# Conditioning vectors of the first feed-forward in column quarters instead of halves

## The chip, the cores and the metric

The kernel runs on one core of a Trainium2 chip. The metric is the device time of one execution in microseconds (us); the time given for a kernel is the median of its runs. A profile is of one execution, taken by the hardware profiler. Engines: PE multiplies matrices, DVE and ACT work on vectors, POOL too, SP issues the loads to the DMA engines.

## The reference

One inference step of a two-layer decoder trunk for a prompt group of 512 tokens and a sample group of 8 sequences of 4 tokens. Each layer is a feed-forward, a mixer and a second feed-forward; each of these three reads a normalised and modulated copy of the residual stream:

```python
mod = (silu(c) @ w_ada[layer] + b_ada[layer]).reshape(Bn, 3, 3, 1024)
u = rmsnorm(h, g_norm[layer, 0]) * (1 + mod[:, 0, 1]) + mod[:, 0, 0]     # scale and shift
h = h + 0.5 * mod[:, 0, 2] * ((silu(a) * b) @ w_down)                      # a, b = split(u @ w_up)
```

`c` is one row per sequence (9 in all), `w_ada` has 1024 rows and 9216 columns. The first feed-forward cannot begin before its shift and scale, two vectors of 1024 numbers for each of the 9 rows, are made from two blocks of `w_ada` of 1024 x 1024 float32 (4.2 MB each).

## The kernel before

The stream `h` lies transposed, as 8 blocks of 128 features by 544 tokens (512 of the prompt, 32 of the samples). Tokens go in two halves of 272. A product is made of three multiplications of float32r parts (high by high, high by low, low by high), lines 176 to 178; the parts are made by a cast on ACT (L157) and a subtraction on DVE (L158). The feed-forward is `ffn_seven`: 22 column blocks of 128 features, each with a pair of weight blocks, one for `a` and one for `b`. The first three column blocks go plainly, one bank of accumulators for each of the pair and each half of the tokens; the rest is done with seven products in place of eight, from sums of operands made on DVE, ACT and POOL. The other function, `ffn`, is called nowhere.

Conditioning vectors are numbered in the order of use; vector 0 is the first shift, vector 1 the first scale. All others go through `ada_steps`: eight loads of 512 KB of 128 full rows (L232), 64 multiplications and a turn (a copy by ACT, two transposes by PE, the addition of the bias and the like by DVE in `set_mods`), handed out one step at a time by `tick` in the feed-forwards. Their loads go into the four buffers of `ada_tile`. Vectors 0 and 1 are made in halves of their columns, `ada_half_loads` (L278), `ada_half` (L288) and `ada_half_turn` (L294 and L296): four loads of 512 KB for one half of one vector, in pieces of 512 columns (2 KB) of two row blocks. Since the memory of the products is not yet in use, their loads borrow the buffers of the product weights, in the order that the list `slots` names: four of `ada_tile`, four of the high and low parts, two raw ones, four more of the high and low parts, and two of `ada_tile` again.

The order of the work is a planner's: it takes the instructions in the order of the program and with its own costs writes one list for each engine, which that engine then runs in order. The loads are all issued by SP. SP's list at the start is: `c`, the identity, the tokens, the first half of vector 0 (with four small loads between), the pair of weight blocks for column block 0 (L163), the first half of vector 1 (with the other four small loads), the second halves of both, then the first four loads of vector 2 (L232), and then the weight pairs for column blocks 1 and 2. The small loads fill `vrow`, which is turned into `vec`, the biases and norm weights that `set_mods` needs.

`first_u(part)` turns one half of both vectors and then makes four blocks of the modulated stream, `make_u`, for both halves of the tokens: a scaling by DVE (L382), the high part by ACT (L401), the low part by DVE (L402), and for the sample tokens a few small operations on DVE, POOL and ACT. With the first half's four blocks, the products of the pair of column block 0 can run over half of their depth; `feed()` then makes the second half, and the rest of the products follows. `tc.issue_after(ready)` holds back the products of the second half of the tokens on the first four blocks until the last conditioning multiplication is issued:

```python
part_of_bank(0, 0)
ready = feed()
with tc.issue_after(ready):
    part_of_bank(1, 0)
for half in range(2):
    part_of_bank(half, 1)
```

There are five banks for products; the pair takes four. The conditioning products of both halves lie in one bank of their own, at different columns.

Of the kernel before, what the change touches and what calls it, by code (L numbers as in the profile page):

```python
# [99 lines left out]
def trunk_kernel(ctx: ExitStack, tc: tile.TileContext, a, out, dbg=None, stop=None):  # L100
# [171 lines left out]
    def ada_half_loads(v, part, slots, between=None):  # L272
        w2d, c0 = ada_cols(v)
        c0 += 512 * part
        ts = []
        for k in range(0, NB, 2):
            t = slots.pop(0)(f"adah{v}_{part}_{k}")[:, 0:1024].rearrange("p (k c) -> p k c", k=2)
            SP.dma_start(out=t, in_=w2d[k * P:(k + 2) * P, c0:c0 + 512].rearrange("(k p) c -> p k c", p=P))  # L278
            ts.append(t)
            if between:  # L280
                between()
        return ts

    def ada_half(v, part, ts, ps):
        o = P * (2 * part + v)
        for k in range(NB):
            for j in range(4):
                mm = PE.matmul(ps[32 * j:32 * j + 32, o:o + P], lhsT=sc[:, k, :], rhs=ts[k // 2][:, k % 2, j * P:(j + 1) * P], start=k == 0, stop=k == NB - 1)  # L288
        return mm

    def ada_half_turn(v, part, ps):
        o = P * (2 * part + v)
        rows = ap_.tile([P, 256], F32, tag="adar", name=f"adahr{v}_{part}")
        S.copy(rows[:, 0:P], ps[:, o:o + P])  # L294
        pt = aux_bank(f"adaht{v}_{part}")
        PE.transpose(pt[:, 0:P], rows[:, 0:P], ident)  # L296
        b = 8 * v + 4 * part
        set_mods(v, 4 * part, 4, mods[:, b:b + 4, :], pt[:, 0:P].rearrange("p (j r) -> p j r", j=4)[:, :, 0:9],
                 vec[:, b:b + 4].unsqueeze(2).to_broadcast([P, 4, 9]))
# [125 lines left out]


    def ffn(name, l, s, gate, after_half, steps=(), final=False, first=None, held=()):
        wu = a["w_ffn_up"][l, s]
        wd = a["w_ffn_down"][l, s]
        steps, held = list(steps), list(held)  # L430
        total, ticks = len(steps), [0]

        def tick():
            ticks[0] += 1
            due = total * ticks[0] // (2 * NQ) - (total - len(steps))
            for _ in range(due):
                steps.pop(0)()

        with tc.tile_pool(name="ffn" + name, bufs=1) as fp:
            gt, wt = {}, {}  # L440

            def up_tiles(q):
                if q not in gt:
                    if q not in wt:
                        wt[q] = (split_cols(f"ua{name}_{q}", wu, q * P), split_cols(f"ub{name}_{q}", wu, FF + q * P))
                    gt[q] = (fp.tile([P, T], F32R, tag="gh", name=f"gh{name}_{q}", bufs=6),
                             fp.tile([P, T], F32R, tag="gl", name=f"gl{name}_{q}", bufs=6))

            def up(q, half):
                up_tiles(q)  # L450
                pa = mm_bank(f"pa{name}_{q}_{half}")
                apply_u(pa, wt[q][0], half)
                pb = mm_bank(f"pb{name}_{q}_{half}")
                apply_u(pb, wt[q][1], half)
                gated(q, half, pa, pb)

            def gated(q, half, pa, pb):
                t0, t1 = HALF[half]
                g = fp.tile([P, HA], F32, tag="g", name=f"g{name}_{q}_{half}", bufs=3)
# [5 lines left out]
            def down(qs, last):  # L465
                wd2 = {}
                for q in qs:
                    _, hi, lo = split(f"wd{name}_{q}", lambda raw: [(raw[:, 0:D], wd[q * P:(q + 1) * P])], D)
                    wd2[q] = (hi, lo)
# [1457 lines left out]
```

## Time and profile before

| what | value |
|---|---|
| median of three runs | 2356.05 us (2349.58 to 2356.92) |
| the profiled execution | 2357.5 us |
| its span | 2355.7 us |
| mean granted clock of PE | 0.988 |
| DMA over the span | 319.43 MB, mean 136 GB/s |
| loads of vectors 0 and 1 (L278) | 16 of 512 KB |

A row of the order of time reads: start, duration, engine, line of the kernel, operation, what is written from what is read, shape, count, and in brackets how long the engine stood idle before it and what ended that. SPq is the queue of loads on SP; its duration is that of the issue, with what it waited for inside a group, and not of the transfer. A busy share of PE near full says that PE had instructions at work, not that it ran at its peak. The granted clock is a share of full speed.

### The profile page before, as it was taken

The page shows a single profiled execution, that of the slowest core. Times are in us where ns is not written, and L with a number is a line of the kernel's source. Part 1 is how long each engine was busy: PE and PEld are TensorE (multiplying, and loading weights), DVE is VectorE, ACT ScalarE, POOL GpSimd, SP SyncE. Part 2 cuts the span into 40 slices and gives each one's busy share as a digit, 9 for nine tenths or more (in the row PEclk, how much of TensorE's full clock was granted, in tenths as well). Part 3 has the DMA queues.
Part 4 walks back from the last instruction along what each step waited for, and adds up shares of the span by engine and source line. Part 5 has one row for each costly group of instructions (what it writes and reads, how often), then busy time and mean ns, then how long its engine had stood idle before and what let it go on. Part 6 is the DMA issues. An engine that isn't in the chain of part 4 may idle for free. (4 is left out here: it accounts for less than half of the span.)

```text
span 2355.7 us, 48935 instructions
## 1 busy us (share of the span) xinstructions
PE 2282.2 (97%) x19292; PEld 2129.1 (90%) x19292; DVE 1740.4 (74%) x3785; ACT 977.8 (42%) x1815; POOL 906.8 (38%) x912
## 2 busy tenths in 40 slices
PE   7999999998999999999989999999998999999999
PEld 6899999997979999999868999999896679999999
DVE  6877677639556976777695977888766767977785
ACT  3333333434533443333523444344436654444432
POOL 0354544206202354553232355552324222465541
PEclk8999999999999999999999999999999999999999
DMA  9545555322263436555458333233147741332331
GB/s 312 175 126 193 195 194 191 108 68 59 61 190 89 141 96 199 190 177 185 153 190 254 102 97 106 86 102 113 48 104 175 232 126 43 91 103 88 100 99 66
DMA packets 356635, 319.43 MB, mean 136 GB/s; under 512 B 24991, under 2 KB 317693, under 8 KB 356358
## 3 DMA queue, kind: packets, MB, share of 16 engines
q1 hardware_dynamic: 341478, 300.24, 40.7%
q0 software_dynamic: 14928, 16.06, 2.8%
q8 instruction: 152, 2.49, 0.4%
q14 instruction: 77, 0.63, 0.1%
HBM read 298.17 MB, written 18.38 MB: 134 GB/s over the span
## 5 line engine op out<-in xcount | busy, mean ns | idle before, releaser
L178 PE MATMUL pd<-gh,ld 128*128 128x272 f32 x1408 | 405.9, 288 | 2.3 <-DVE ld L158 2.3
L176 PE MATMUL pd<-gh,hd 128*128 128x272 f32 x1408 | 406.9, 289 | 1.4 <-ACT gh L157 1.4
L177 PE MATMUL pd<-gl,hd 128*128 128x272 f32 x1408 | 406.3, 289 | 1.6 <-DVE gl L158 1.2
L176 PE MATMUL p<-uh,hu 128*128 128x272 f32 x1216 | 351.5, 289 | 0.0
L178 PE MATMUL p<-uh,lu 128*128 128x272 f32 x1216 | 350.8, 288 | 0.0
L177 PE MATMUL p<-ul,hu 128*128 128x272 f32 x1216 | 350.4, 288 | 0.0
L178 PEld LDWEIGHTS pd<-gh,ld 128*128 128x128 f32 x1408 | 265.4, 189 | 3.0 <-DVE ld L158 3.0
L177 PEld LDWEIGHTS pd<-gl,hd 128*128 128x128 f32 x1408 | 265.6, 189 | 2.8 <-DVE gl L158 1.6
L176 PEld LDWEIGHTS pd<-gh,hd 128*128 128x128 f32 x1408 | 265.6, 189 | 2.1 <-ACT gh L157 1.6
L176 PE MATMUL p<-th,hu 128*128 128x272 f32 x912 | 264.2, 290 | 0.0
L178 PE MATMUL p<-th,lu 128*128 128x272 f32 x912 | 263.8, 289 | 0.0
L177 PE MATMUL p<-tl,hu 128*128 128x272 f32 x912 | 262.8, 288 | 0.0
L408 DVE SCALAR_TENSOR_TENSOR h<-pd,mods,h 128x272 f32<-128x272 f32 (+1 forms) x448 | 212.3, 478 | 68.0 <-PE pd L178 66.6
L158 DVE TENSOR_TENSOR lu<-rua,hu 128x512 fp32r<-128x512 f32 (+1 forms) x228 | 232.9, 1022 | 35.6 <-ACT hu L157 32.4
L157 ACT CAST hu<-rua 128x512 fp32r<-128x512 f32 (+1 forms) x228 | 173.8, 762 | 180.1 <-PE p L177 105.3
L176 PEld LDWEIGHTS p<-uh,hu 128*128 128x128 f32 x1216 | 229.3, 189 | 5.4 <-issue 2.9
L649 POOL TENSOR_TENSOR s<-rua,rub 128x512 f32<-128x512 f32 x76 | 121.1, 1593 | 286.8 <-DMA rub<-in_w_ffn_up_dram 154.0
L177 PEld LDWEIGHTS p<-ul,hu 128*128 128x128 f32 x1216 | 229.4, 189 | 0.0
L178 PEld LDWEIGHTS p<-uh,lu 128*128 128x128 f32 x1216 | 229.0, 188 | 0.0
L413 POOL TENSOR_TENSOR h<-h,gs 128x32 f32<-128x32 f32 x224 | 114.3, 510 | 244.8 <-DVE gs L411 228.5
L655 POOL TENSOR_TENSOR rua<-rub,rua 128x512 f32<-128x512 f32 x76 | 108.2, 1424 | 186.0 <-DVE lu L158 108.3
L176 PEld LDWEIGHTS p<-th,hu 128*128 128x128 f32 x912 | 171.8, 188 | 4.9 <-issue 2.5
(543 smaller groups left out, 5953.8 us busy)
## 6 DMA issues: line engine op xcount, KB each, us to landing
adaw<-in_w_ada_dram SPq DMA_DIRECT2D x128, 512.0 KB, 6.1
rua<-in_w_ffn_up_dram SPq DMA_DIRECT2D x88, 512.0 KB, 4.3
rub<-in_w_ffn_up_dram SPq DMA_DIRECT2D x88, 512.0 KB, 3.9
rd<-in_w_ffn_down_dram SPq DMA_DIRECT2D x96, 384.0 KB, 3.4
adah<-in_w_ada_dram SPq DMA_DIRECT2D x16, 512.0 KB, 6.1
adaw<-in_w_ada_kv_dram SPq DMA_DIRECT2D x16, 512.0 KB, 7.1
rd<-in_w_ffn_down_dram SPq DMA_DIRECT2D x16, 512.0 KB, 3.5
kp<-in_cache_k_dram SPq DMA_DIRECT2D x16, 512.0 KB, 9.8
```

The costliest lines, as they stand in the source:

```text
L157: S.copy(hi, src)
L158: V.tensor_tensor(out=lo, in0=src, in1=hi.bitcast(F32), op=ALU.subtract)
L176: PE.matmul(ps, lhsT=wh, rhs=xh, start=first and i == 0, stop=False)
L177: PE.matmul(ps, lhsT=wh, rhs=xl, start=False, stop=False)
L178: PE.matmul(ps, lhsT=wl, rhs=xh, start=False, stop=last and i == n - 1)
L408: V.scalar_tensor_tensor(out=h[:, m, t0:p1], in0=ps[:, 0:n], scalar=mods[:, gate + m, 0:1], in1=h[:, m, t0:p1], op0=ALU.mult, op1=ALU.add)
L413: G.tensor_tensor(out=h[:, m, TP:T], in0=h[:, m, TP:T], in1=st[:], op=ALU.add)
L649: G.tensor_tensor(out=o["s3"][:], in0=a11, in1=a21, op=ALU.subtract)
L655: G.tensor_tensor(out=a11, in0=a21, in1=a11, op=ALU.subtract)
```

## The change

Vectors 0 and 1 are made in four parts of 256 columns, and each part of both vectors is followed by its own two blocks of the modulated stream and its part of the products of the first pair.

- Loads: two of 512 KB for one part of one vector, four row blocks of 256 columns each (pieces of 1 KB). The first parts of both vectors come ahead of the first weight pair, with all eight small loads between them; the second parts come behind it, and the third and fourth are issued behind `first_u(0)` in the program. The list of borrowed buffers is put in another order: four of `ada_tile`, eight of the high and low parts, two raw ones, two of `ada_tile`.
- Multiplications: 128 as before, on 64 rows of the accumulators and not 128. Odd parts go into a second bank, taken from the five for products.
- Turn: one copy of 64 rows for both vectors, two transposes of 64 rows, `set_mods` twice on two blocks.
- Order: the part n+1 of the conditioning stands in the program ahead of the products on part n; `issue_after` is gone.
- `ffn`, which nothing calls, is deleted.

```diff
-    def ada_half_loads(v, part, slots, between=None):
+    def ada_part_loads(v, part, slots, between=()):
+
         w2d, c0 = ada_cols(v)
-        c0 += 512 * part
+        c0 += 256 * part
         ts = []
-        for k in range(0, NB, 2):
-            t = slots.pop(0)(f"adah{v}_{part}_{k}")[:, 0:1024].rearrange("p (k c) -> p k c", k=2)
-            SP.dma_start(out=t, in_=w2d[k * P:(k + 2) * P, c0:c0 + 512].rearrange("(k p) c -> p k c", p=P))
+        for k in range(0, NB, 4):
+            t = slots.pop(0)(f"adah{v}_{part}_{k}")[:, 0:1024].rearrange("p (k c) -> p k c", k=4)
+            SP.dma_start(out=t, in_=w2d[k * P:(k + 4) * P, c0:c0 + 256].rearrange("(k p) c -> p k c", p=P))
             ts.append(t)
-            if between:
-                between()
+            for f in between:
+                f()
         return ts
...
-    def ada_half(v, part, ts, ps):
-        o = P * (2 * part + v)
+    def ada_part(v, part, ts, ps):
+        o = P * (2 * (part // 2) + v)
         for k in range(NB):
-            for j in range(4):
-                mm = PE.matmul(ps[32 * j:32 * j + 32, o:o + P], lhsT=sc[:, k, :], rhs=ts[k // 2][:, k % 2, j * P:(j + 1) * P], start=k == 0, stop=k == NB - 1)
-        return mm
...
+            for j in range(2):
+                PE.matmul(ps[32 * j:32 * j + 32, o:o + P], lhsT=sc[:, k, :], rhs=ts[k // 4][:, k % 4, j * P:(j + 1) * P], start=k == 0, stop=k == NB - 1)
+
+    def ada_part_turn(part, ps):
+        o = 2 * P * (part // 2)
+        rows = ap_.tile([P, 256], F32, tag="adar", name=f"adahr{part}")
+        S.copy(rows[0:64], ps[0:64, o:o + 256])
+        pt = aux_bank(f"adaht{part}")
+        for v in range(2):
+            PE.transpose(pt[:, 64 * v:64 * v + 64], rows[0:64, v * P:(v + 1) * P], ident[0:64, 0:64])
+        for v in range(2):
+            b = 8 * v + 2 * part
+            set_mods(v, 2 * part, 2, mods[:, b:b + 2, :], pt[:, 64 * v:64 * v + 64].rearrange("p (j r) -> p j r", j=2)[:, :, 0:9],
+                     vec[:, b:b + 2].unsqueeze(2).to_broadcast([P, 2, 9]))
...
-                part_of_bank(0, 0)
-                ready = feed()
-                with tc.issue_after(ready):
-                    part_of_bank(1, 0)
-                for half in range(2):
-                    part_of_bank(half, 1)
+                for k0 in range(0, NB, 2):
+                    if k0 + 2 < NB:
+                        feed(k0 // 2 + 1)
+                    for half in range(2):
+                        for i in range(2):
+                            apply_u(banks[half][i], wt[0][i], half, k0, k0 + 2)
...
-    slots = [ada_tile] * 4 + [lo32, hi32] * 2 + [raw_tile] * 2 + [lo32, hi32] * 2 + [ada_tile] * 2
-    ps0 = app.tile([P, 512], F32, tag="ada", name="ada01")
+    slots = [ada_tile] * 4 + [lo32, hi32] * 4 + [raw_tile] * 2 + [ada_tile] * 2
+    ps0 = [app.tile([P, 512], F32, tag="ada", name="ada01")]
 
     def first_u(part):
-        for v in range(2):
-            ada_half_turn(v, part, ps0)
+        if part:
+            for v in range(2):
+                ada_part(v, part, early[part][v], ps0[part % 2])
+        ada_part_turn(part, ps0[part % 2])
         for hf in range(2):
-            make_u(f"00{part}", hf, mod(0, 0, 0), mod(0, 0, 1), 4 * part, 4 * part + 4)
+            make_u(f"00{part}", hf, mod(0, 0, 0), mod(0, 0, 1), 2 * part, 2 * part + 2)
...
-    early = [ada_half_loads(0, 0, slots, small_load)]
+    early = [[ada_part_loads(v, 0, slots, [small_load] * 2) for v in range(2)]]
     wu0 = a["w_ffn_up"][0, 0]
     w00 = (split_cols("ua00_0", wu0, 0), split_cols("ub00_0", wu0, FF))
-    early.append(ada_half_loads(1, 0, slots, small_load))
-    late = [ada_half_loads(v, 1, slots) for v in range(2)]
+    early.append([ada_part_loads(v, 1, slots) for v in range(2)])
     for v in range(2):
-        ada_half(v, 0, early[v], ps0)
+        ada_part(v, 0, early[0][v], ps0[0])
...
-    def feed():
-        for v in range(2):
-            mm = ada_half(v, 1, late[v], ps0)
-        first_u(1)
-        return mm.ins
+    ps0.append(mm_bank("ada01b"))
+    for part in range(2, 4):
+        early.append([ada_part_loads(v, part, slots) for v in range(2)])
...
-              seq0[:-2] + [late_consts, late_masks], first=(w00, feed), held=seq0[-2:], slots=5, late=True)
+              seq0[:-2] + [late_consts, late_masks], first=(w00, first_u), held=seq0[-2:], slots=5, late=True)
```

More of the change, by code (lines that the diff above doesn't have):

```diff
@@ L291, in ada_half_turn @@
[L291 to L299, printed above, removed]
+            for j in range(2):
+                PE.matmul(ps[32 * j:32 * j + 32, o:o + P], lhsT=sc[:, k, :], rhs=ts[k // 4][:, k % 4, j * P:(j + 1) * P], start=k == 0, stop=k == NB - 1)
@@ L761, in ffn_seven @@
                 banks = [[mm_bank(f"p{x}{name}_0_{half}") for x in "ab"] for half in range(2)]
-                def part_of_bank(half, part):
-                    for i in range(2):
-                        apply_u(banks[half][i], wt[0][i], half, 4 * part, 4 * part + 4)
-                part_of_bank(0, 0)
-                ready = feed()
-                with tc.issue_after(ready):
-                    part_of_bank(1, 0)
-                for half in range(2):
-                    part_of_bank(half, 1)
+                for k0 in range(0, NB, 2):
[4 more added lines that the diff above has]
+                            apply_u(banks[half][i], wt[0][i], half, k0, k0 + 2)
                 for half in range(2):
```

78 lines of the change are left out of this document (removed).

## The prediction

> **What bounds it now.** I read the page first, then busy time by stretch, then the order of time near the start, engine by engine.
>
> ```profile
> PE 2282.2 (97%) x19292; PEld 2129.1 (90%) x19292; DVE 1740.4 (74%) x3785; ACT 977.8 (42%) x1815; POOL 906.8 (38%) x912
> ...
> 0.00:31.00 31.00, 18.77 (x208) 14.48 (x208) 18.08 (x49) 8.51 (x15) 1.10 (x6) 0.83 0.97 335
> 31.00:51.00 20.00, 19.72 (x214) 16.99 (x218) 15.46 (x39) 10.35 (x24) 0.91 (x2) 0.92 0.88 286
> 51.00:100.00 49.00, 45.32 (x388) 41.25 (x388) 45.74 (x90) 20.64 (x42) 12.02 (x10) 0.97 0.67 219
> 100.00:2355.70 2255.70, 2198.40 (x18489) 2056.35 (x18487) 1661.14 (x3609) 938.28 (x1737) 892.74 (x895) 0.99 0.42 130
> ```
>
> In the rows by stretch the columns are the stretch, its length, the busy time of PE, its weight loads, DVE, ACT and POOL, the granted clock, the DMA share and GB/s. Over the run PE is the bound (97%). The edit touches only the first 51 us and what starts from there. Up to 31 us PE has 31 - 18.77 = 12.2 us free and the DMA engines have none (0.97). From 31 to 51 PE has 0.3 us free: that is the first pair. From 51 to 100 DVE is as full as PE (45.74 and 45.32 of 49).
>
> The order of time from the last conditioning load to the second pair:
>
> ```profile
> 17.07 10.11 SPq L278 DMA_DIRECT2D adah<-in_w_ada_dram  x12
> 26.42 0.64 PE L288 MATMUL ada<-adah,sc 128*32 128x128 f32 x16 [1.56 <-DMA adah<-in_w_ada_dram]
> 31.05 0.59 PE L176 MATMUL pa<-uh,hua 128*128 128x272 f32 x1 [0.91 <-ACT uh L401]
> 36.77 2.82 PE L288 MATMUL ada<-adah,sc 128*32 128x128 f32 x94
> 39.71 0.27 ACT L294 COPY adahr<-ada 128x128 f32<-128x128 f32 x1 [3.51 <-PE ada L288]
> 40.39 0.27 ACT L294 COPY adahr<-ada 128x128 f32<-128x128 f32 x1 [0.42 <-PE adaht L296]
> 41.54 1.75 DVE L382 SCALAR_TENSOR_TENSOR nv<-h,mods,rb 128x272 f32<-128x272 f32 x3
> 48.26 0.84 DVE L402 SCALAR_TENSOR_TENSOR ul<-nv,mods,uh 128x240 fp32r<-128x240 f32 x2
> 50.68 0.28 PE L178 MATMUL pb<-uh,lub 128*128 128x272 f32 x1
> 52.75 0.39 PE L176 MATMUL pa<-uh,hua 128*128 128x272 f32 x1
> ```
>
> The first half's last load reaches PE at 26.42, the first product runs at 31.05, the second half's conditioning products end at 39.59 (36.77 + 2.82), its second turn starts at 40.39, its modulation runs on DVE from 41.54 to 49.10, and the pair's last product ends at 50.96. So the end of the pair is set by the modulation of four blocks in both token halves (7.56 us on DVE) behind the second half's turn, and not by PE's own work.
>
> ```profile
> 34.00:36.00 2.00, 2.00 (x21) 1.73 (x20) 1.82 (x6) 0.95 (x3) 0.00 (x0) 0.91 1.04 411
> 36.00:38.00 2.00, 2.00 (x56) 1.77 (x52) 0.70 (x2) 0.20 (x1) 0.00 (x0) 1.00 0.67 269
> 38.00:40.00 2.00, 2.00 (x61) 1.75 (x53) 0.00 (x0) 0.27 (x1) 0.00 (x0) 1.00 0.08 27
> ```
>
> DMA is full until about 37.4 (36 plus 0.67 of 2) and then empty until 40: the second half's data are there some 2 us before PE has finished with them. That slack pays for the slower loads below.
>
> **The change, part by part.** *Loads.* 16 loads of 512 KB stay 16, but a piece is 1 KB long and no longer 2 KB. The DMA view of three stretches: 20 to 36 us (the halves, 2 KB), 632.5 to 633.5 (loads of 1 KB pieces), 676 to 677.5 (mostly 512 B).
>
> ```profile
> DMA packets 3201, 6.42 MB, mean 401 GB/s; under 512 B 199, under 2 KB 199, under 8 KB 3198
> DMA packets 364, 0.37 MB, mean 373 GB/s; under 512 B 0, under 2 KB 364, under 8 KB 364
> DMA packets 748, 0.49 MB, mean 326 GB/s; under 512 B 15, under 2 KB 748, under 8 KB 748
> ```
>
> The 8.39 MB (16 x 524,288 B) take 20.9 us at 401 and 22.5 at 373: 1.6 us more. Ends: 0 at 401, and 4.8 at 326 (25.7). I take 1.6, the row with the same piece. The 2 us of slack hide it, so the last quarter is read by PE at about 39.6 as now: term 0, from -1.6 to +3.2. One quarter (2.1 MB) then comes every 5.6 us. SP issues the same number; the four small loads that stood behind the first weights now stand ahead of them. The first weights' casts wait for ACT and not for their data, as the next rows show.
>
> ```profile
> 11.95 0.37 SPq L163 DMA_DIRECT2D rua<-in_w_ffn_up_dram  x1
> 13.37 2.66 SPq L1036 DMA_DIRECT2D vrow<-in_g_norm_dram  x1
> 21.36 0.40 ACT L354 COPY rb<-rb0b 128x288 f32<-128x288 f32 x1 [1.88 <-PE rb0b L352]
> 21.65 1.05 ACT L157 CAST hua<-rua 128x1024 fp32r<-128x1024 f32 x1
> ```
>
> A stall of 2.66 us moves the issue from 11.95 to 14.6; the queue holds some 4.5 MB up to there (issued by 12, about 335 GB/s), so no bubble follows: 0, or at most 2.7 if it did.
>
> *Start.* Only 2.1 MB of conditioning, and no longer 4.2, stand ahead of the first modulation, but the norm's factors are in place only at 21.76 (21.36 + 0.40). The first product can run at 24 at best (a scaling, an activation and the cast of hua after that) and at 28 if DVE keeps the two splits of the first weights and the vector copy ahead of it. I take 25. PE's work from the first product to the end of the pair is 50.96 - 31.05 = 19.9 us now, almost without a gap; from 25 it would end at 44.9, from 24 at 43.9, from 28 at 47.9. These are floors for the sum.
>
> *Turns.* Two in sequence at the end take 41.54 - 39.59 = 1.95 us; one copy of 64 rows for both vectors, two short transposes and three DVE operations take its place. I estimate 1.7 (a second turn begins 0.68 after the first): -0.3, from -0.7 to +0.3. Over all, DVE gets six operations of about 0.2 us and ACT and POOL a few short ones more, 1.2 us while DVE waits for DMA; hidden under a quarter's 5.6 us (its modulation is 3.8), and 1.2 if that cover were gone.
>
> *Modulation.* After the last turn stand two blocks and not four: 7.56 / 2 = 3.8 us less. Ends: 3.8, and 2.5 if DVE is still busy with the third quarter. *Products.* 24 and not 48 remain; the tail after the last modulation (49.10 to 50.96) stays. In the code the third quarter's products come behind the fourth's conditioning products, so they fill the fourth turn. *Order and banks.* PE takes its list in order, and without the old rule on the order a quarter's conditioning products may stand ahead of the quarter before's products and hold them until the loads land. At the last quarter this costs nothing: a quarter of PE's 19.9 us behind 39.6 ends at 44.6, ahead of DVE's last modulation at 45.3. The fifth product bank, which the odd quarters' conditioning products now take, is free again after the last turn's copy, before the second pair asks for it: 0; held a whole modulation longer it would cost that pair at most 3.8. The function that goes is not called. Sum for the pair: 0 - 0.3 - 3.8 = -4.1, end at 46.9, which is above PE's floor of 44.9.
>
> *Second pair.* Its loads stand on SP behind four loads of the next vector, two of which wait for the slots of the last quarter as they wait for the last half now:
>
> ```profile
> SPq L232 <- PE ada L288: 3.8, 1, 3.8
> 41.14 0.39 SPq L163 DMA_DIRECT2D rua<-in_w_ffn_up_dram  x1
> 41.62 0.94 SPq L163 DMA_DIRECT2D rub<-in_w_ffn_up_dram  x1
> 48.44 1.03 ACT L157 CAST hua<-rua 128x1024 fp32r<-128x1024 f32 x1
> 50.89 1.93 PE L242 MATMUL ada<-adaw,sc 128*32 128x256 f32 x30
> 51.55 1.22 DVE L158 TENSOR_TENSOR lub<-rub,hub 128x1024 fp32r<-128x1024 f32 x1
> DMA to landing us min/median/max: 6.4/6.4/6.4
> DMA to landing us min/median/max: 7.6/7.6/7.6
> ```
>
> (The last two are the tiles rua and rub in the first 50 us.) With the release at the same time they are issued at 41.14 and 41.62 again and land at 47.5 and 49.2. Then a cast and a split, 1.03 + 1.22, make the first usable at 49.8, and 1.05 + 1.22 the second at 51.5. PE has 1.93 us of the next vector's products first, until 48.8, begins the pair at about 49.2 and needs the low part soon after: 52.75 - 49.2 = 3.5 us gained of 4.1. From here on a pair's weights hold PE as much as PE itself; if they came 2 us later, 1.5 would be left.
>
> Sum: -4.1 + 0.6 = -3.5. The profiled execution took 2357.5 us (span 2355.7 and 1.8 around it), which gives 2354.0; that execution lies 1.45 above the median of the three, 2356.05, so a median is 2352.5.
>
> *A rule that speaks against it.* The clock rows by stretch: 0.83 up to 31 us, 0.92 from 31 to 51, and this finer one:
>
> ```profile
> 32.00:34.00 2.00, 2.00 (x15) 1.62 (x9) 2.00 (x6) 1.14 (x3) 0.00 (x0) 0.50 1.06 406
> ```
>
> The Trainium skill, page "TensorE: Matmul & The Clock Gate", Part 1, says that the array falls to half clock after an idle window of about 3.4 us and needs a busy one to rise. The trace agrees (0.50 while the first products run). By the rule at its worst, two more cold windows between quarters at half rate take 1.7 us each of PE, an estimate from that page: 3.4 on the floor of 44.9, an end at 48.3, and the sum would be about -2.5. By the rows a quarter's gap is only 5.6 less 19.9 / 4 = 0.6 us, so I add nothing.
>
> **Rivals.** (1) *Short pieces cost nothing.* PE then finishes the last quarter 1.6 us sooner, SP's release comes 1.6 sooner, and the whole gain is 3.5 + 1.6 = 5.1: 2350.9. For it: the row at 373 stands on 0.37 MB of another tensor within 1 us. Against it: the three rows fall in the order of their pieces, 401, 373, 326. The Trainium skill, page "DMA: Bandwidth & Descriptors", Specifications, gives 512 B as the smallest transfer at line rate; this trace differs (326 against 401).
>
> (2) *The gain is given back before 100 us.* DVE is busy for 45.74 of 49 us, and PE waits there for splits:
>
> ```profile
> 85.08 0.39 PE L178 MATMUL pd<-gh,ld 128*128 128x272 f32 x1 [1.39 <-DVE ld L158]
> 89.83 0.39 PE L176 MATMUL pd<-gh,hd 128*128 128x272 f32 x1 [1.35 <-ACT gh L157]
> 90.00:95.00 5.00, 4.27 (x24) 4.06 (x25) 4.77 (x11) 2.10 (x5) 0.60 (x1) 0.74 0.42 120
> ```
>
> If DVE, fed by loads that come no sooner, ends this stretch when it does now, 0 to 1 us is left: 2355.5. Against it: DVE itself is free 3.8 us earlier, with operations on the modulated blocks ready to run.
>
> (3) *Slower: DVE collides with POOL.* Beside POOL's work on the later weights, DVE operations stretch:
>
> ```profile
> 72.10 1.36 POOL L655 TENSOR_TENSOR rua<-rub,rua 128x512 f32<-128x512 f32 x1
> 72.25 2.97 DVE L556 TENSOR_TENSOR x<-uh,ul 128x272 f32<-128x272 f32 x2
> 76.91 0.79 DVE L556 TENSOR_TENSOR x<-uh,ul 128x272 f32<-128x272 f32 x2
> ```
>
> Two operations took 2.97 us beside POOL and 0.79 alone: 2.2 us for one meeting. A DVE that runs ahead while POOL's start stays with its load meets it at other operations. It decides from two further meetings (4.4 against 3.5 gained); three cost 6.6 and give 2356.05 + 3.1 = 2359.2. For it: this stretch has such a meeting in a full DVE; against it: nothing makes the new order meet POOL more often than the old one.
>
> **How the numbers follow.** Forecast 0.45 (its own range 2349 to 2356), rival 1 0.15, rival 2 0.22, rival 3 0.18. The three runs of before spread by 7.3 us (2349.58 to 2356.92), so a measurement of this kernel tells no less than about 0.3%, 7.1 us, from no change. Faster by more than that is out of reach of the sum and takes scatter on top of the gain: 0.16 (a sixth of the forecast, a third of rival 1, a little of the others). Slower by it: 0.10 (a third of rival 3, a tenth of rival 2). Within: 0.74. The range takes in rival 1's best and rival 3: 2346 to 2360.
>
> **What would show it.** In the changed profile: the first product at 24 to 28 us and not 31; conditioning loads with pieces of 1 KB and their DMA stretch at about 373 GB/s; PE's last conditioning product at 39 to 40; DVE's last modulation near 45.3; the pair's last product near 47; the second pair's first product near 49.2; the granted clock at 1.0 between quarters from about 30. It is wrong if the last quarter is read after 41, if the second pair starts with 52 or later, or if the same work after 100 us takes a different time.

## The result, and the profile after

The changed kernel takes 2359.76 us (median of 22 runs, 2352.22 to 2371.1); the kernel before, run beside it, 2354.11 us (22 runs, 2348.16 to 2362.94). The ratio is 1.0027, with a 95% interval of 1.0017 to 1.0036: some 6 us longer, where 3.5 us less were forecast. The time lies inside the range of 2346 to 2360, but the direction is the wrong one. The ratios in this document are taken over fast runs alone, without one slow run of e6 (2477.59 us) and one of e10 (3118.17 us) that the medians below include, so a ratio can differ from the quotient of its two medians. The profiled execution took 2359.2 us, with a span of 2357.4.

The busy time of each engine over the span, from the first part of the page of the kernel after:

```profile
PE 2284.2 (97%) x19296; PEld 2131.8 (90%) x19296; DVE 1743.5 (74%) x3795; ACT 977.4 (41%) x1817; POOL 910.0 (39%) x916
```

Over the run nothing has changed: PE 2284.2 us against 2282.2. The busy time by stretch of the kernel after (columns as in the prediction):

```profile
0.00:31.00 31.00, 20.28 (x176) 16.98 (x177) 20.02 (x57) 9.62 (x16) 0.88 (x6) 0.89 0.97 320
25.00:30.00 5.00, 4.41 (x42) 3.74 (x44) 4.12 (x8) 1.81 (x4) 0.00 (x0) 0.50 1.10 356
31.00:51.00 20.00, 20.00 (x232) 17.80 (x231) 12.73 (x33) 8.00 (x17) 2.97 (x6) 1.00 0.87 285
```

From 31 to 51 us PE is now busy for all of the 20 us (19.72 before), and DVE for less than before (12.73 against 15.46). The forecast had DVE's modulation as the last thing to wait for; the profile says that PE is the bound, and at 19.72 of 20 us it nearly was so before. From 25 to 30 us PE runs at half clock. What PE does there, in order of time:

```profile
25.59 5.15 PE L289 MATMUL ada01b<-adah,sc 128*32 128x128 f32 x48 [2.96 <-DMA adah<-in_w_ada_dram]
30.67 0.39 PE L176 MATMUL pa<-uh,hua 128*128 128x272 f32 x1
30.99 1.07 PE L289 MATMUL ada01b<-adah,sc 128*32 128x128 f32 x16
...
35.53 3.69 PE L289 MATMUL ada<-adah,sc 128*32 128x128 f32 x64
...
42.82 3.69 PE L289 MATMUL ada01b<-adah,sc 128*32 128x128 f32 x64
...
50.12 1.05 PE L242 MATMUL ada<-adaw,sc 128*32 128x256 f32 x10
...
56.77 0.29 PE L178 MATMUL pb<-uh,lub 128*128 128x272 f32 x1
56.99 1.05 PE L242 MATMUL ada<-adaw,sc 128*32 128x256 f32 x10
57.97 0.39 PE L176 MATMUL pa<-uh,hua 128*128 128x272 f32 x1
```

Two things stand in these rows. First, a quarter's 64 conditioning multiplications take 3.69 us, 58 ns each; before, 94 of the same shape took 2.82 us, 30 ns each. Second, the first product runs at 30.67, no earlier than before (31.05), because the second quarter's multiplications stand ahead of it in PE's list and wait 2.96 us for their data. The pair's last product ends at 57.06 (56.77 + 0.29) and not at 50.96, and the second pair begins at 57.97 and not at 52.75.

The same view for SP and for DVE:

```profile
14.88 16.74 SPq L279 DMA_DIRECT2D adah<-in_w_ada_dram  x12
...
22.67 0.26 DVE L205 TENSOR_TENSOR mods<-adaht,vec 128x18 f32<-128x18 f32 x2
23.18 1.48 DVE L384 SCALAR_TENSOR_TENSOR nv<-h,mods,rb 128x272 f32<-128x272 f32 x3
...
47.64 0.26 DVE L205 TENSOR_TENSOR mods<-adaht,vec 128x18 f32<-128x18 f32 x2 [0.88 <-PE adaht L297]
47.93 0.18 DVE L217 SCALAR_TENSOR_TENSOR mods<-mods,vec 128x18 f32<-128x18 f32 x1
48.04 1.23 DVE L158 TENSOR_TENSOR lub<-rub,hub 128x1024 fp32r<-128x1024 f32 x1
49.18 1.00 DVE L384 SCALAR_TENSOR_TENSOR nv<-h,mods,rb 128x272 f32<-128x272 f32 x2
```

And the DMA view from 28 to 40 us:

```profile
DMA packets 4141, 4.52 MB, mean 377 GB/s; under 512 B 138, under 2 KB 3886, under 8 KB 4139
```

DVE has the first quarter's factors at 22.67 and scales at 23.18: the modulation starts as early as forecast. The loads come at 377 GB/s, as forecast for 1 KB pieces (373). But the twelve loads of SP's row are not in the order of the program. The planner's list for SP has two loads of vector 0's *fourth* quarter first (they go into the raw buffers, which are free at once), and then the second quarter's four. Two loads of 512 KB at 377 GB/s are 2.8 us, an estimate, that the second quarter comes later.

How far the rest of the run is shifted can be read from one instruction that all kernels have: the squares for the norm behind the first feed-forward, on ACT. Before and after:

```profile
442.00 0.43 ACT L361 ACTIVATE sq<-h 128x272 f32<-128x272 f32 x1 [3.56 <-POOL h L413]
```

```profile
445.62 0.43 ACT L363 ACTIVATE sq<-h 128x272 f32<-128x272 f32 x1 [3.56 <-POOL h L415]
```

So 3.6 us of the 5.2 at the second pair are left at 442 us. The two spans differ by 1.7 us only. The profiled execution of before ran a stretch at a lower clock a little later, which after's did not, and its 3.4 us of full clock are enough to account for the difference; the rows from 455 to 465 us of before:

```profile
455.00:460.00 5.00, 4.18 (x24) 3.89 (x25) 4.29 (x13) 2.63 (x6) 1.15 (x6) 0.76 0.80 230
460.00:465.00 5.00, 5.00 (x28) 3.94 (x28) 3.44 (x18) 0.00 (x0) 0.00 (x0) 0.56 0.50 202
```

The same two rows of after have a clock of 1.00. One execution of each is thus not enough for a difference of some us at the end of the run. The row at 442 us lies ahead of that stretch, but it isn't free of such differences either: up to 31 us the granted clock is 0.83 in before, 0.89 in after, 0.94 in e10 and 1.00 in e11, and 0.17 of 31 us is 5.3 us of full clock.

### The profile page after: what moved, and what is told of

Its sections match the earlier page's. It is cut to its first block, busy times and chain, and to the rows that moved or that the text cites. A ratio compares the mean times of both kernels' runs of the same rounds, so it can differ in the third digit from the quotient of the medians.

```text
span 2357.4 us, 48958 instructions
## 1 busy us (share of the span) xinstructions
PE 2284.2 (97%) x19296; PEld 2131.8 (90%) x19296; DVE 1743.5 (74%) x3795; ACT 977.4 (41%) x1817; POOL 910.0 (39%) x916
## 5 line engine op out<-in xcount | busy, mean ns | idle before, releaser
L157 ACT CAST hu<-rua 128x512 fp32r<-128x512 f32 (+1 forms) x228 | 173.9, 763 | 183.8 <-PE p L177 111.3
```

Of the source, the lines that this page charges most:

```text
L157: S.copy(hi, src)
```

## The experiments

Eleven kernels. In the table, the pair's end is the end of its last product, and the next columns are the second pair's first product and the ACT row above, as its distance from 442.00. "Beside" is the kernel before in the same group of runs. The traces are of one execution each; only one kernel was profiled twice, as e6 and e10, and these two lie 0.5 us apart at 442 us and 0.8 us at the pair's end. In e4 the products of the two pairs are mixed, so that two of its cells are empty.

| kernel | median, us | beside | ratio (95% interval) | pair ends | second pair | at 442 us |
|---|---|---|---|---|---|---|
| before | 2354.11 | | | 50.96 | 52.75 | 0 |
| after | 2359.76 | 2354.11 | 1.0027 (1.0017 to 1.0036) | 57.06 | 57.97 | +3.6 |
| e1 four row groups | 2352.88 | 2353.82 | 0.9997 (0.9987 to 1.0007) | 51.48 | 53.27 | -2.9 |
| e2 before, two row groups | 2358.87 | 2353.82 | 1.0018 (1.0005 to 1.0031) | 53.01 | 54.79 | +1.1 |
| e3 before, 1 KB pieces | 2355.85 | 2353.82 | 1.0011 (0.9999 to 1.0024) | 53.05 | 54.83 | +1.9 |
| e4 products first | 2365.72 | 2353.82 | 1.0047 (1.0035 to 1.0059) | | | +5.2 |
| e5 e1 and PE's order | 2351.33 | 2351.99 | 0.9998 (0.9984 to 1.0011) | 50.67 | 52.46 | -1.0 |
| e6 e5 and SP's order | 2352.63 | 2351.99 | 0.9991 (0.9977 to 1.0005) | 49.55 | 52.01 | -3.4 |
| e7 after with SP's order | 2355.7 | 2351.99 | 1.0007 (0.9992 to 1.0022) | 55.24 | 56.59 | +0.8 |
| e8 e6, buffers freed earlier | 2353.12 | 2351.99 | 0.9994 (0.998 to 1.0009) | 51.22 | 53.01 | -2.4 |
| e9 e8 without PE's order | 2361.79 | 2352.84 | 1.0032 (1.0017 to 1.0048) | 56.55 | 65.06 | +6.4 |
| e10 e6 again | 2353.85 | 2352.84 | 0.9995 (0.998 to 1.0009) | 50.37 | 52.34 | -2.9 |
| e11 e6 on two row groups | 2356.26 | 2352.84 | 1.0008 (0.9991 to 1.0026) | 51.59 | 52.94 | -3.5 |

### e1: the change, on four row groups

A multiplication here has 32 columns of conditioning against 128 of weights, and its result takes 32 rows of a bank. Before, the rows 0, 32, 64 and 96 took turns, four column blocks of one vector; after, a quarter has two column blocks and only the rows 0 and 32 are used. e1 puts the second vector at the rows 64 and 96, and nothing else differs in the program but that one copy and one transpose do for both:

```diff
-    def ada_part(v, part, ts, ps):
-        o = P * (2 * (part // 2) + v)
+    def ada_part(part, ts, ps):
+        o = P * (part // 2)
         for k in range(NB):
-            for j in range(2):
-                PE.matmul(ps[32 * j:32 * j + 32, o:o + P], ...)
+            for v in range(2):
+                for j in range(2):
+                    r = 64 * v + 32 * j
+                    PE.matmul(ps[r:r + 32, o:o + P], ...)
```

> The changed kernel with one edit: the multiplications of both vectors for one quarter go to all four groups of 32 rows (64 v + 32 j) in turn and not to two, so one copy of 128 rows and one transpose follow. Theory A (on two groups of rows the same 64 instructions take twice the PE time, 3.69 us and not 1.9, and PE is the bound from 25 to 57 us): 64 instructions in about 1.9 us, last product of the first pair at 48 to 52 and not 57, time 4 to 8 us under the changed kernel and 0 to 4 us under the kernel before. Theory B (the order of PE's list, with conditioning ahead of products, or the loads hold it): within 1.5 us of the changed kernel, so about 4 to 6 us over the kernel before.

Measured: 2352.88 us, ratio 0.9997, where the change has 1.0027: some 7 us less (0.0030 of 2354). In order of time on PE:

```profile
26.79 0.41 PE L291 MATMUL ada01b<-adah,sc 128*32 128x128 f32 x4 [3.04 <-DMA adah<-in_w_ada_dram]
27.13 0.39 PE L176 MATMUL pa<-uh,hua 128*128 128x272 f32 x1
...
36.30 0.39 PE L176 MATMUL pa<-uh,hua 128*128 128x272 f32 x1 [0.78 <-ACT uh L404]
...
42.47 1.94 PE L291 MATMUL ada01b<-adah,sc 128*32 128x128 f32 x60
```

Sixty multiplications take 1.94 us, 32 ns each. The wait for the second quarter is as long as after the change (3.04 against 2.96), and still the loss is gone. But two things differ in the trace: the rate, and PE's list as the planner makes it, in which twelve products stand behind the first four multiplications of the second quarter, so that the first product runs at 27.13 and not at 30.67. e1 shows that the step to two row groups brings on the loss, together with the list that comes of it; it doesn't show how much of the loss is the rate by itself. e10 and e11, below, ask that. The Trainium skill, page "TensorEngine Tiling (Array Packing)", Performance Considerations, says that a left operand of 32 columns allows a four-fold tiling of the array's columns. The trace agrees: 30 to 32 ns with four places in turn, 58 ns with two.

### e2: the kernel before, neighbours on two row groups

The other way round: the kernel before, with its loop in blocks of eight multiplications that stay on two row groups.

```diff
-        for k in range(NB):
-            for j in range(4):
+        for k, j in [(k0 + k, j0 + j) for k0 in range(0, NB, 4) for j0 in (0, 2) for k in range(4) for j in range(2)]:
...
```

> The kernel before with one edit: in each half of a vector the multiplications go to row groups 0 and 1 for four row blocks and then to groups 2 and 3, so that neighbours in the list share two groups and not four. Nothing else moves. Theory A: the block of conditioning ahead of the second half's turn takes 5.0 to 5.6 us for 94 instructions and not 2.82, the first pair ends 2 to 4 us later, time 1.5 to 4 us over the kernel before. Theory B: no change, within 1 us.

Measured: 2358.87 us, ratio 1.0018 (1.0005 to 1.0031), longer, as expected, but the trace bears out less of it:

```profile
38.22 3.43 PE L287 MATMUL ada<-adah,sc 128*32 128x128 f32 x94
```

94 multiplications in 3.43 us are 36 ns each, and not 58, so the block of 5.0 to 5.6 us that was expected did not come. A reason would be that a block of eight on one pair of groups overlaps with the next eight on the other; no run separates this. The pair ends 2.0 us later than before, and 1.1 us are left at 442 us, against 4.2 by the ratio and 5.1 by the medians. The direction is shown, the size is not explained by the trace.

### e3: the kernel before, with 1 KB pieces

```diff
-        for k in range(0, NB, 2):
-            t = slots.pop(0)(...)[:, 0:1024].rearrange("p (k c) -> p k c", k=2)
-            SP.dma_start(out=t, in_=w2d[k * P:(k + 2) * P, c0:c0 + 512]...)
+        for k, q in ((0, 0), (0, 1), (4, 0), (4, 1)):
+            t = slots.pop(0)(...)[:, 0:1024].rearrange("p (k c) -> p k c", k=4)
+            SP.dma_start(out=t, in_=w2d[k * P:(k + 4) * P, c0 + 256 * q:c0 + 256 * q + 256]...)
...
```

> The kernel before with one edit: each of the 16 loads of the first two vectors takes four row blocks of 256 columns (pieces of 1 KB) and not two of 512 (2 KB); multiplications, turns and order as before. Theory A: the loads end 1 to 2 us later, which the slack before the second half's turn hides: within 1.5 us of the kernel before. If short pieces are what costs the changed kernel its time: 3 to 6 us over the kernel before.

Measured: 2355.85 us, ratio 1.0011 (0.9999 to 1.0024): level, or up to some 6 us longer. The DMA view of the stretch from 20 to 36 us:

```profile
DMA packets 5942, 5.95 MB, mean 372 GB/s; under 512 B 183, under 2 KB 5930, under 8 KB 5940
```

And the stretch from 20 to 30 us of e3, then of before:

```profile
20.00:30.00 10.00, 7.70 (x96) 5.02 (x96) 3.38 (x6) 2.82 (x5) 0.00 (x0) 0.50 1.08 369
```

```profile
20.00:30.00 10.00, 7.70 (x107) 5.23 (x106) 4.56 (x10) 2.82 (x5) 0.66 (x2) 0.67 1.05 401
```

The rate is what was forecast, 372 GB/s against 401. The trace is 1.9 us late at 442 us; but PE also ran this stretch at 0.50 of its clock, where the execution of before had 0.67: 1.7 us of full clock in 10. Whether slower loads or this clock made the 1.9 us can't be told from one execution.

### e4: products ahead of the next quarter's conditioning

The change, with two lines moved: a quarter's products stand in the program ahead of the next quarter's conditioning.

```diff
-                    if k0 + 2 < NB:
-                        feed(k0 // 2 + 1)
                     for half in range(2):
                         for i in range(2):
                             apply_u(banks[half][i], wt[0][i], half, k0, k0 + 2)
+                    if k0 + 2 < NB:
+                        feed(k0 // 2 + 1)
```

> The changed kernel with one edit: in the program the products on quarter n stand ahead of the conditioning of quarter n+1, and no longer behind it. Theory A (PE's work is too much, whatever its order): first product earlier, at 24 to 28 us, but the pair's end not before 54, and 2 to 6 us over the kernel before. Theory B (the order of PE's list is the cause): the pair ends at 51 or earlier, time equal to the kernel before or under it.

Measured: 2365.72 us, ratio 1.0047 (1.0035 to 1.0059), the slowest. Its first product in order of time:

```profile
24.53 0.39 PE L176 MATMUL pa<-uh,hua 128*128 128x272 f32 x1 [1.80 <-ACT uh L403]
```

And PE's waits from 20 to 110 us (total, times, longest):

```profile
PE pd L178 <- DVE ld L158: 4.4, 1, 4.4
PE pa L176 <- ACT uh L403: 2.7, 3, 1.8
PE pa L177 <- DVE ul L404: 1.4, 1, 1.4
```

The first product does run early, at 24.53, but the quarters' products now wait for their own modulation with the conditioning behind them: 2.7 + 1.4 = 4.1 us in the two lower rows. The upper row is a wait at 95 us, past the first pairs. Theory A had the early product, but the time is longer than either theory said: some 6 us over the change by the medians, 1.6 us by the row at 442 us. So the order of PE's list can cost as much as the whole change did; the trace bears out the smaller figure.

### e5, e6, e7: PE's order, SP's order, and both

e5 is e1 with the rule of the kernel before on the order, by quarters: the products of quarter n stand behind the last conditioning multiplication of quarter n+1. e7 is the change with SP's loads in the order of use, by another order of borrowed buffers. e6 has e5's rule and e7's order.

```diff
 e5
-                    if k0 + 2 < NB:
-                        feed(k0 // 2 + 1)
+                    with ExitStack() as order:
+                        if k0 + 2 < NB:
+                            order.enter_context(tc.issue_after(feed(k0 // 2 + 1)))
 e6, e7
-    slots = [ada_tile] * 4 + [lo32, hi32] * 4 + [raw_tile] * 2 + [ada_tile] * 2
+    slots = [ada_tile] * 4 + [raw_tile] * 2 + [lo32, hi32] * 4 + [ada_tile] * 2
```

> The kernel of e1 (four groups of rows) with one rule on the order added: the products on quarter n may be issued only after the last conditioning multiplication of quarter n+1, as the kernel before had it for its halves. The loads stay in the order of the changed kernel. If PE's list, which in e1 puts a quarter's conditioning behind products that wait for a modulation, holds back the turns: the pair ends at 48 to 50 and not 51.5, time 1 to 3 us under e1 and under the kernel before. If it is loads alone that hold e1: within 1 us of e1.

> The kernel of e5 with the loads in the order 1, 2, 3, 4 as in e7. This is the change as the prediction took it: conditioning at 0.03 us an instruction, loads in order, products of quarter n filling the turn of quarter n+1. By the prediction's own sum the pair ends at 46 to 47 and the time is 3 to 5 us under the kernel before; if the gain is given back between 50 and 100 us, 0 to 1 us under it.

> The changed kernel with one edit in the list of borrowed buffers: the two raw buffers serve the second quarter and no longer the fourth, with which SP issues the quarters in the order 1, 2, 3, 4 (in the changed kernel the fourth quarter's two loads of vector 0 stand ahead of the second quarter's four). Two groups of rows as in the changed kernel. If the theory that the half rate on two groups is most of the loss holds: the second quarter's 1.05 MB come 2.7 us sooner, PE starts its closed run 2 to 3 us sooner and is still the bound; the pair ends at 54 to 55 and not 57; time 1 to 3 us under the changed kernel, 2 to 5 over the kernel before. If the load order is the whole loss: level with the kernel before or under it.

Measured: e7 2355.7 us, ratio 1.0007 (0.9992 to 1.0022), against 1.0027 for the change. The order of the loads alone is worth 2 us by the medians (3.7 over before against 5.65), 2.8 by the rows at 442 us and 4.7 by the ratios, whose intervals overlap. Its rows on PE:

```profile
24.91 3.40 PE L289 MATMUL ada01b<-adah,sc 128*32 128x128 f32 x48
28.24 0.39 PE L176 MATMUL pa<-uh,hua 128*128 128x272 f32 x1
```

The second quarter's multiplications no longer wait for data, and the first product runs 2.4 us sooner (28.24 against 30.67), though the first turn of this execution came 2.2 us later (24.51 against 22.30). e5 is at 2351.33 us, 0.9998, level with e1: the rule on PE's order brings nothing by itself that these intervals show, while the loads are late. e6 is at 2352.63 us, 0.9991 (0.9977 to 1.0005). Its rows on PE and SP:

```profile
40.69 1.95 PE L291 MATMUL ada01b<-adah,sc 128*32 128x128 f32 x64
...
43.84 0.39 SPq L163 DMA_DIRECT2D rua<-in_w_ffn_up_dram  x1
...
49.27 0.28 PE L178 MATMUL pb<-uh,lub 128*128 128x272 f32 x1
...
52.01 0.39 PE L176 MATMUL pa<-uh,hua 128*128 128x272 f32 x1 [0.59 <-ACT hua L157]
53.27 0.40 PE L178 MATMUL pa<-uh,lua 128*128 128x272 f32 x1 [0.74 <-DVE lua L158]
```

This is the change as it was meant, but it doesn't reach what was expected of it, an end of the pair at 46 to 47 and 3 to 5 us less than before: the pair ends at 49.55, 1.4 us sooner than before, and then the second pair's weights are late. They were issued at 43.84 (41.14 before), and PE waits 0.59 and 0.74 us for their cast and their split. At 442 us the trace is 3.4 us ahead. Most of that lead was not made in the first pair, since the second pair begins only 0.7 us sooner (52.01 against 52.75). It came later; the stretch from 80 to 100 us of before, and then of e6:

```profile
80.00:100.00 20.00, 16.53 (x116) 15.88 (x115) 17.97 (x37) 7.77 (x15) 6.43 (x6) 0.91 0.41 120
```

```profile
80.00:100.00 20.00, 18.57 (x144) 17.92 (x143) 19.82 (x39) 8.77 (x16) 7.65 (x6) 1.00 0.43 128
```

PE is busy there for 2 us more than in before and loses nothing to the clock, where before loses 1.8 us (0.09 of 20). The clock in this stretch is 1.00 in e1, e6, e8 and e10, which are 2.4 to 3.4 us ahead at 442 us, and 0.91 in e5, which is 1.0 ahead. Whether an earlier pair brings the full clock there or the execution happened to have it can't be told from these traces.

### e8: the buffers of the last quarter freed earlier

e6, with the third quarter in the two last `ada_tile` and two of the high and low parts, so that the second pair's loads can go out sooner.

```diff
-    slots = [ada_tile] * 4 + [raw_tile] * 2 + [lo32, hi32] * 4 + [ada_tile] * 2
+    slots = [ada_tile] * 4 + [raw_tile] * 2 + [lo32, hi32] * 2 + [ada_tile] * 2 + [lo32, hi32] * 2
```

> The kernel of e6 with the buffers of vector 2's loads given to the third quarter and not to the fourth, so that these loads, and the second pair's weights behind them on SP, need not wait for the fourth quarter. If the second pair's weights hold PE after the first pair: second pair's first product 1 to 3 us sooner than in e6 and the time 1 to 2 us under it. If PE or DVE hold it: within 1 us of e6.

Measured: 2353.12 us, 0.9994 (0.998 to 1.0009), level with e6. In order of time on PE and SP:

```profile
32.63 0.33 PE L299 MATMUL adaht<-cst,adahr 128*128 128x128 f32 x1 [2.61 <-ACT adahr L297]
...
39.46 0.38 SPq L163 DMA_DIRECT2D rua<-in_w_ffn_up_dram  x1
```

The weights are issued 4.4 us sooner than in e6, but in this execution the second quarter's turn waits 2.61 us for its copy on ACT, which stands behind a modulation, and the pair ends later (51.22) and the second begins at 53.01, not the 1 to 3 us sooner that early weights would have given. e10, below, has the same wait without this edit, so it doesn't belong to it.

### e9: four row groups and early loads, without the rule on PE's order

e1 with the buffers of e8.

> The changed kernel with the conditioning multiplications on four row groups, the four quarters' loads issued in the order of their use, the third quarter in the buffers that come free first, and no rule on the order of PE's list. Theory A (row groups and load order were the whole fault, and a rule on PE's order isn't needed): the pair's last product at 50.0 us or sooner, the second pair's first at 51.5 or sooner, 2 to 4 us less than before at 100 to 400 us, the run 2350 to 2352. Theory B (PE's order matters by itself): products that wait for their modulation are placed ahead of conditioning multiplications whose loads have landed, the pair ends at 51 or later, and the run is level with before, 2352 to 2355.

Measured: 2361.79 us, ratio 1.0032 (1.0017 to 1.0048): longer than before, which neither theory said. PE and SP in order of time:

```profile
31.51 26.46 SPq L232 DMA_DIRECT2D adaw<-in_w_ada_dram  x8
58.02 0.42 SPq L163 DMA_DIRECT2D rua<-in_w_ffn_up_dram  x1
...
65.06 0.59 PE L176 MATMUL pa<-uh,hua 128*128 128x272 f32 x1 [1.11 <-ACT hua L157]
```

The planner, with its own costs, put eight loads of the next vector into SP's list ahead of the second pair's weights; these wait for buffers, and the weights behind them are issued at 58.02 and not at 39.46, as in e8 with the same buffers. The second pair starts at 65.06. The products that wait for their modulation come on top, as PE's waits from 20 to 110 us show:

```profile
PE pa L176 <- ACT uh L404: 3.7, 4, 1.5
```

### e10 and e11: four and two row groups, side by side

e10 is e6 once more; e11 is e6 with the multiplications of the change, on two row groups, and with two short transposes.

> The kernel with four row groups, the rule on PE's order and the loads in order of use, a second time, beside its two-group twin. Theory A: in the trace 3 to 4 us less than before at 100 to 400 us, as in its first profile, and a median 1 to 4 us under before. Theory B (the first trace's 3.4 us were the scatter of one execution at the start): 0 to 1 us at 100 to 400 us, and a median level with before.

> The same kernel with the conditioning multiplications on two row groups again, as the change has them, and nothing else different. Theory A (PE's rate is a cost by itself, whatever the orders): a block of 64 at 3.6 to 3.7 us and not 1.95, three such blocks inside the pair, so the pair ends 4 to 5.5 us later than with four groups, and the run is 4 to 5.5 us longer than that of four groups beside it, 2 us over before. Theory B (the orders were the fault, the rate was hidden under the loads): within 1 us of four groups.

Measured: 2353.85 us (0.9995) and 2356.26 us (1.0008). e10's trace is 2.9 us ahead at 442 us, as e6's was, which goes with theory A; its time is level with before, as theory B has it. e11 is 2.4 us longer than e10 by the medians, less than the 4 to 5.5 expected and within the intervals of both. e11 in order of time on PE, and then e10:

```profile
22.36 0.33 PE L298 MATMUL adaht<-cst,adahr 64*128 64x64 f32 x2 [0.20 <-ACT adahr L295]
...
39.82 3.69 PE L289 MATMUL ada01b<-adah,sc 128*32 128x128 f32 x64
```

```profile
24.59 0.33 PE L299 MATMUL adaht<-cst,adahr 128*128 128x128 f32 x1
...
31.76 0.33 PE L299 MATMUL adaht<-cst,adahr 128*128 128x128 f32 x1 [2.60 <-ACT adahr L297]
```

Their rows from 31 to 51 us, e11 and then e10:

```profile
31.00:51.00 20.00, 20.00 (x224) 18.01 (x223) 13.80 (x38) 8.17 (x21) 1.60 (x5) 1.00 0.85 283
```

```profile
31.00:51.00 20.00, 19.24 (x240) 17.59 (x244) 15.56 (x46) 8.50 (x23) 2.04 (x6) 0.91 0.82 273
```

A block takes 3.69 us again, and PE is full; but PE, always busy, kept its clock at 1.00, where e10 lost 0.09 of 20 us, 1.8 us, to half clock behind its waits (as much as one block costs), and this execution of e11 also came to its first factors 2.2 us sooner than e10's (a first turn at 22.36 against 24.59). So at 442 us no loss is left in this trace. With the other two repairs in place, the rate costs about 2.4 us by the medians, and not 5; the intervals allow for none. And e11, still on two row groups, is at 1.0008 where the change is at 1.0027: the two orders alone are worth 0.0019, or 4.5 us, though these intervals overlap too. So the repair of the row groups alone (e1) and that of the orders alone (e11) each take away most of the loss. They don't add up, and the runs don't split the loss between them.

### Where the repaired change ends

Five runs of repaired kernels (e1, e5, e6, e8, e10) are 1.0 to 3.4 us ahead at 442 us in their traces, and their ratios lie between 0.9991 and 0.9998, each with 1 in its interval. None is shown to beat the kernel before. Part of it may be taken back later: the stretch from 700 to 760 us has a clock of 1.00 in the profiles of before, of after and of e7, and of 0.97 in all five (1.8 us each). In e6 it is 0.81 from 745 to 750 us and 0.84 from 750 to 755, where before has 1.00 in both. But e2, e9 and e11 show 0.96 to 0.97 there as well, and two of these are late and not early. Whether the earlier end of the first feed-forward causes it stays open: one execution of each kernel can't tell it.

## Why the prediction was wrong

*What bounds it.* The prediction read that "the end of the pair is set by the modulation of four blocks" and "not by PE's own work". The second of these did not hold even for the kernel before. DVE's modulation did end late, at 49.10 us, with PE's last ten products right behind it, but PE was as full as DVE was late: it was busy for 19.72 of 20 us from 31 to 51 us, and behind its first product the profile lists no wait of PE for a modulation. A modulation shorter by 3.8 us could by itself have brought the end forward by some 0.9 us (0.28 us idle and 0.62 us of the next vector's multiplications), an estimate; the rest of the 4.1 had to come from a start of PE that is sooner, with no more to do. In the change PE had more to do: DVE is less busy from 31 to 51 us and PE is full.

*Loads.* The rate was right: 377 GB/s in the change and 372 in e3, with 373 forecast. But the sentence "the last quarter is read by PE at about 39.6 as now: term 0" failed: it was read at 46.5 (42.82 + 3.69), and not for the data, which were there, but for PE's list. Even in e6, with both orders and the rate as meant, it was read at 42.64 (40.69 + 1.95).

*Start.* The factors were there in time (22.67, scaling at 23.18), so a first product near 25 was possible, and e4 shows one at 24.53. "I take 25" failed since I looked only at what the product needs, and not at what stands ahead of it on PE: the second quarter's 48 multiplications, which waited 2.96 us for data and then took 5.15 us at half clock. The step on the order had named this effect ("may stand ahead of the quarter before's products and hold them until the loads land") and then priced it at the last quarter alone, at nothing. It was due at the first. And I took SP's order from the program, where the planner had put two loads of the fourth quarter first, so that the quarters did not come one by one "every 5.6 us"; e7 prices that at 2 to 5 us.

*PE's floor.* This is the term that was off by most, 6.5 us, where the late start is 5.7 (30.67 against 25): "PE's work from the first product to the end of the pair is 50.96 - 31.05 = 19.9 us now ... from 25 it would end at 44.9". The 19.9 us were carried over unchanged. From first product to the end of the pair the change took 57.06 - 30.67 = 26.4 us. Of the 6.5 more, 4.6 are the conditioning multiplications (1.07 + 3.69 + 3.69 = 8.45 against 0.66 + 0.42 + 2.82 = 3.9), and 2.1 are products of the next vector that moved into the pair (1.05 + 1.05 + 0.62 against 0.62). With this floor, even a start at 25 would have ended at 51.4, later than before. That is still too kind: 48 multiplications of the second quarter ran ahead of 30.67 and would have stood behind a start at 25, 2.8 us more at 58 ns, an estimate. The diff showed `32 * j` with j up to 2 in place of 4, and the row of before showed 30 ns for an instruction of 128 columns; that the one depends on the other was not asked. The row that would have priced it does not exist in the trace of before, where all conditioning runs on four groups, though a hint did: there one multiplication takes 272 ns or more and the next starts some 30 ns on, so several are under way at once. The rate should then have been bounded from both sides, by one and by two times 30 ns.

*Turns and modulation.* The last turn took 1.6 us, from 46.51 to the factors at 48.11 (47.93 + 0.18), with 1.7 forecast. Then a split of the second pair's weights (1.23 us at 48.04) stood ahead of the modulation, which began at 49.18; two blocks, not four, were left, as said. None of it decided anything beside a PE that was later still.

*Second pair.* The weights did set its start in e6 (waits of 0.59 and 0.74 us), as "a pair's weights hold PE as much as PE itself" had it; in the change PE was later still, and the first of the weights were issued as early as 33.47, because the planner put only two of the next vector's loads ahead of them.

*Sum.* The forecast of -3.5 looks like what the traces of e6 and e10 show at 442 us, -3.4 and -2.9, once the two premises (the rate and the orders) are made true by other edits. That is chance: there the pair ends 1.4 and 0.6 us sooner and not 4.1, the second pair begins 0.7 and 0.4 us sooner and not 3.5, and the rest of the lead comes from the stretch up to 100 us, which the sum had at nothing. Their medians don't confirm a gain that outlasts the run.

*Rivals.* The price of the third rival, 2359.2, is the time that came out, but its mechanism (DVE meeting POOL) had no part in it: the loss was there with the second pair at 58 us, ahead of the stretch (from 72 us) where that rival placed it. "Given back before 100 us" was not it either; in e6 and e10 that stretch added to the lead. The rule on the clock, weighed and left out, did bear on it: the clock was 0.50 from 25 to 30 us, behind PE's wait for the second quarter, and the 48 multiplications took 107 ns each there (5.15 / 48). The trace of before agreed with that rule only in part: its 0.50 from 32 to 34 us stands behind waits of 1.56 and 0.91 us, shorter than the idle window that the rule names. The places named as the ones that would show the prediction wrong came true in two of three cases: the last quarter was read after 41, and the second pair began later than 52. The work after 100 us took the same time, as far as 442 us: the change is 3.9 us behind at the cast on ACT (L157) at 98 us of before, and 3.6 at 442.

What is left over: the trace accounts for 3.6 us at 442 us, the medians for some 6. e2 has a similar gap. It was not settled.

## What to carry to other kernels

Before a block of work is split, ask what the engine's rate depended on: small multiplications that took turns over four places of the array ran at twice the rate of the same ones over two, and PE had no room for the difference. When PE is busy for 19.7 of 20 us and waits for nothing, a shorter chain on another engine doesn't bring its end forward. When work is cut into pieces that come in sequence, write down for each queue what stands ahead of the first piece's consumer, from the list that the planner makes and not from the program; three of the kernels here (the change, e4, e9) lost by such an order about what the split could bring, or more. A floor carried over from the old profile is only as good as the claim that each instruction in it keeps its price.

## What the runs showed of the hardware

The rate of the 32-column multiplications: 30 to 32 ns each in turn over four row groups, 58 ns over two, 36 ns over two with a change of the pair after every eight, and 107 ns over two at half clock. Four groups at 30 ns and two at 58 both make some 120 ns between two multiplications of one group, an estimate from these rows. Whether that time belongs to a group's part of the array or to its accumulators was not separated, since each edit changed both. Loads mostly in pieces of 1 KB ran at 372 to 377 GB/s in two kernels (the change and e3) and of 2 KB at 401.

A wait of 2.96 us on PE went with a stretch at half clock in the change (0.50 from 25 to 30 us), so that a late load cost its wait and then part of the work behind it. In e11, whose longest wait from 20 to 51 us was 0.95 us, the clock stayed at 1.00.
